# A mixer trunk whose emission planner models TensorE's clock: new branch order and two attention workers

## The chip, the core and the metric

One core of a Trainium2 chip runs the whole program. The time is device microseconds of one execution, the median of three runs. TensorE multiplies 128x128 tiles, VectorE (DVE) and ScalarE (ACT) work elementwise, GpSimd (POOL) does some elementwise work and accumulating DMAs, SyncE (SP) starts the plain DMAs. Each engine takes its instructions strictly in the order in which the program lists them.

## What is computed

Two layers. In each, five branches read the normalised input: a (differential attention), b (dilated attention), c (a diagonal state recurrence, S5), d (compressed, selected and window attention), e (attention into a memory). The outputs are gated, projected, weighted and summed, and a last projection is added to the residual.

```python
for l in range(DEPTH):
    h = rmsnorm(x, norm_g[l])
    proj = h @ w_in[l]            # q, k, v and gate columns of a, b, c, d, e
    ...
    o_a = diff_attention(qa, ka, va, lam, lam_init, diff_subln_g[l])
    o_b = dilated_attention(qb, kb, vb)
    o_c = s5_branch(c_u, ...)
    o_d = nsa_attention(d_q, d_kc, d_vc, d_ks, d_vs, d_kw, d_vw, d_g, ...)
    o_e = memory_attention(e_q, mem, mem_norm_g[l], w_mem_kv[l])
    branches = jnp.stack([o_a * jax.nn.silu(a_z), ..., o_e * jax.nn.silu(e_z)], axis=2)
    y = jnp.einsum('bsnc,ncd->bsnd', branches, w_branch[l])
    gate = jax.nn.sigmoid(h @ w_merge[l] + b_merge[l])
    x = x + (jnp.einsum('bsnd,bsnd->bsd', gate, y)) @ w_out[l]
return rmsnorm(x, final_g)
```

There are 512 tokens of width 1024, 256 memory tokens, four heads of 64 in each attention branch.

## The kernel before

Tokens lie along the free axis, channels along the 128 partitions, so nearly every tile is 128x512. Each float32 operand is split into a high part (a rounded copy) and a low part (the rest), and a product is three matmuls: `mm3` issues high x high, low x high, high x low into one accumulator. A projection of 128 channels is eight such triples, 24 matmuls of 512 columns into an `acc` tile (a PSUM bank). Weights come as pieces of 128x512: a SyncE DMA into `raw`, a ScalarE cast into `whi`, and `wlo` either as a VectorE subtraction or as a ScalarE negated copy to which a GpSimd DMA adds the weights again.

An attention head makes scores in an `sc` tile piece by piece (`causal_exp`: VectorE masks and finds the maximum, ScalarE takes the exponential into `prob`), normalises `prob` on VectorE, and then (`pv`) for three groups of blocks transposes `prob` on TensorE into `pt`, copies it to `ph` on ScalarE, takes the rest `pl` on VectorE, and multiplies both with the values into `o`. `pt` and `ms` (small sums) share the three `sc` buffers. There are three `acc`, three `sc` and two `o` buffers. The compression of d (`compress`, tiles `cxh`, `hd`) takes weight pieces too, but uses a piece up in four narrow matmuls. The recurrence (`s5_operators`, tiles `e`, `p`, `c`) is a chain of small VectorE steps with a few TensorE products (`ms<-e,c`). The memory's keys and values are `mem_kv` (`mh`, `ml`).

The order of all this is not written out. `_trace` runs generators, called streams: the attention workers, the compression, the recurrences, the projections, the trunk (gates, branch projections, output projection) and the memory. It runs first without emitting, to list weight pieces and grants of buffers, then again to emit. Each instruction advances an estimated clock of its engine (`_Engine`, line 223). TensorE's clock `T.now` is the program's: `_Streams.run` (line 321) picks the first stream, by rank, whose wake time has been reached, or else the one that wakes first. So the estimate decides the order in which instructions stand in each engine's queue. Line 243 records every instruction, which is why every row of the profile has L243.

The constants of line 39 on steer it: `ORDER` and `MERGES` list the branches of each layer for the projections and for the trunk, `AFTER` says what the recurrence (`c`) and the memory of layer 1 (`m`) wait for, `RANK` orders the streams, `WORKERS` is the number of heads that may run at once, `PA` holds how many heads of d (or of a's first half) may be left when a projection of a starts, two numbers for each layer.

Of the kernel before, what the change touches and what calls it, by code (L numbers as in the profile page):

```python
# [37 lines left out]
LAT = 100  # L38
ORDER = ('beda', 'edba')
MERGES = ('bedac', 'edbca')  # L40
AFTER = {'s': 'mem', 'c': ('mem', 'dk'), 'm': ('b', 'a')}
RANK = {'att': 1, 'cmp': 1, 'rec': 2, 'ch': 3, 'proj': 4, 'trunk': 5, 'mem': 3}
EARLY = (1, 1)
GO = 4
WORKERS = 3
PA = (4, 4, 2, 4)

MAGIC = 12582912.0
SQ2PI = math.sqrt(2.0 / math.pi)
# [176 lines left out]
class _Engine:  # L226


    def __init__(self, eng, ready, clock, per, fixed):
        self.eng, self.ready, self.clock, self.per, self.fixed = eng, ready, clock or self, per, fixed  # L230
        self.now = 0.0

    def __getattr__(self, name):
        def call(out, *args, **kw):
            ins = [a for a in (*args, *kw.values()) if hasattr(a, "tensor")]
            n = max(math.prod(a.shape[1:]) for a in [out] + ins)
            start = max([self.now, self.clock.now] + [self.ready.get(a.tensor.name, 0.0) for a in ins])
            self.now = start + self.cost(name, n, out, args) + (190 if "accum_out" in kw else 0)
            outs = [out, args[-1]] if name == "tensor_tensor_reduce" else [out, kw.get("accum_out", out)]
            for a in outs:  # L240
                self.ready[a.tensor.name] = self.now + LAT
            if self.eng is not None:
                getattr(self.eng, name)(out, *args, **kw)  # L243

        return call

    def cost(self, name, n, out, args):
        return self.fixed + n * (165 if ALU.pow in args else self.per * (1.5 if name == "tensor_tensor_scan" else 1))


class _Tensor(_Engine):
    def cost(self, name, n, out, args):
        n = math.prod(out.shape[1:])
        if name == "matmul" and args[1].dtype != F32R:
            return 2 * (self.fixed + max(64, 2 * n) * self.per)
        return self.fixed + max(107, n * self.per)


class _Queue(_Engine):
# [150 lines left out]
def _trace(ctx, tc, A, plan):  # L410
# [33 lines left out]
    def take(ring, dt=F32):  # L444
        return rings[AL.get(ring, ring)].take(nm(ring), dt)
# [14 lines left out]
    def slots(n, s, dt=F32R):  # L460
        return [slot(s, dt) for _ in range(n)]
# [16 lines left out]
    def need(*keys):  # L478
        return lambda: all(k in R for k in keys)
# [383 lines left out]

    def mem_kv(l):
        if l == 0:
            yield need("x")
        yield arena.room(18, SPARE)
        raws = slots(4, "mraw", F32)
        for q in range(4):
# [18 lines left out]
        for k in range(KD):  # L888
            yield at(raws[k // 2], cols)
            c = slice(256 * (k % 2), 256 * (k % 2) + 256)  # L890
# [30 lines left out]
        for i in range(2):  # L921
            a = yield from take("acc")
# [10 lines left out]
        for i in range(2):  # L933
            a = yield from take("acc")
# [713 lines left out]
    def s5_operators(l, h):  # L1648
# [43 lines left out]
        def place(b):  # L1692

            x = yield from take("tmp")
            for g in range(4):
                src = bass.AP(kd.tensor, kd.offset + (4 * b + g) * 16 * 240, [[240, 16], [16, 8], [1, 128]])
                SY.dma_start(x[:, 128 * g:128 * g + 128], src)
            yield at(x)
            AC.copy(m2[b].rearrange("p (g c t) -> p g c t", g=4, t=TC), x.rearrange("p (g t c) -> p g c t", g=4, t=TC))
            give("tmp", x, AC.now)  # L1700

        js = [spawn(place(b), RANK["rec"]) for b in range(2)]
        m1 = slots(2, "m1", F32)
# [306 lines left out]
    def memories():  # L2010
        for l in range(L):
            if l:
                yield need(("o", l - 1, "abcde".index(AFTER["m"][l])))
            yield from mem_kv(l)

    def projections():
        for l in range(L):
            yield need(("h", l))
            tabs, which = None, None
            for b in ORDER[l]:  # L2020
# [15 lines left out]
                else:  # L2036
                    for i in range(2):
                        if i == 0 and ORDER[l].index("a") > ORDER[l].index("d"):
                            yield lambda: left.get((l, "d"), 4) <= PA[2 * l]
                        elif i:  # L2040
                            yield lambda: left.get((l, "a", 0), 2) <= PA[2 * l + 1]
                        yield from proj_a(l, i, tabs)
# [9 lines left out]
    def attentions():  # L2052
        while jobs:
            yield from jobs.pop(0)
# [6 lines left out]
    def recurrences():  # L2061
        yield need((AFTER["s"], 0))
        yield from s5_params()
        for l in range(L):
            yield from lambda_params(l)
        for l in range(L):
            yield need((AFTER["c"][l], l) if AFTER["c"][l][0] != "o" else ("o", l, "abcde".index(AFTER["c"][l][1])))
            ys = []
            for h in range(2):
                ops = yield from s5_operators(l, h)  # L2070
                uc = yield from s5_in(l, h)
                ys.append((yield from s5_chunks(l, h, uc, *ops)))
            yield from s5_glu(l, ys)
# [51 lines left out]
    AC.activation(mrep[:, 0:1], mhalf[:, 0:1], AF.Exp)  # L2125
    for _ in range(WORKERS):
        spawn(attentions(), RANK["att"])
    spawn(compression(), RANK["cmp"])
    spawn(recurrences(), RANK["rec"])
    spawn(projections(), RANK["proj"])  # L2130
    spawn(opening(), 1)
    spawn(trunk(), RANK["trunk"])
    spawn(memories(), RANK["mem"])
# [21 lines left out]
```

## Time and profile before

| | us |
|---|---|
| median of three runs (1364.15 to 1365.39) | 1364.4 |
| the profiled execution | 1364.17 |
| its span, first to last instruction | 1362.4 |
| TensorE busy in the span | 1279.9 |
| VectorE busy | 870.1 |
| ScalarE busy | 835.4 |
| GpSimd busy | 407.6 |

The page gives the busy time of each engine. [...] Its waits view sums the idle time of an engine by the tile it was about to write and by the engine and tile it waited for. Its timeline lists single instructions.

### The profile page before, as it was taken

The page shows a single profiled execution, that of the slowest core. Times are in us where ns is not written, and L with a number is a line of the kernel's source. Part 1 is how long each engine was busy: PE and PEld are TensorE (multiplying, and loading weights), DVE is VectorE, ACT ScalarE, POOL GpSimd, SP SyncE. Part 2 cuts the span into 40 slices and gives each one's busy share as a digit, 9 for nine tenths or more (in the row PEclk, how much of TensorE's full clock was granted, in tenths as well). Part 3 has the DMA queues.
Part 4 walks back from the last instruction along what each step waited for, and adds up shares of the span by engine and source line. Part 5 has one row for each costly group of instructions (what it writes and reads, how often), then busy time and mean ns, then how long its engine had stood idle before and what let it go on. Part 6 is the DMA issues. An engine that isn't in the chain of part 4 may idle for free.

```text
span 1362.4 us, 19594 instructions
## 1 busy us (share of the span) xinstructions
PE 1279.9 (94%) x6303; PEld 1051.5 (77%) x6303; DVE 870.1 (64%) x2199; ACT 835.4 (61%) x1699; POOL 407.6 (30%) x523
## 2 busy tenths in 40 slices
PE   5799799999999989999989889999989999999997
PEld 3688677887888778888867567888867888888886
DVE  6978866666787585344457968757877673333442
ACT  6677767757676364644547766757877573434442
POOL 2733323203236235211232354312225222111112
PEclk8999899999999989999989889999989999999998
DMA  7574677736798798676844796656549767656651
GB/s 249 115 164 109 142 188 181 175 95 127 164 187 174 188 202 186 148 189 172 246 112 108 173 218 150 145 128 158 114 113 195 147 139 163 154 133 162 177 171 62
DMA packets 130630, 215.30 MB, mean 158 GB/s; under 512 B 22496, under 2 KB 29792, under 8 KB 130528
## 3 DMA queue, kind: packets, MB, share of 16 engines
q0 software_dynamic: 40896, 74.47, 34.0%
q1 hardware_dynamic: 89632, 139.59, 32.9%
q8 instruction: 49, 0.80, 0.2%
q14 instruction: 53, 0.43, 0.1%
HBM read 190.38 MB, written 23.56 MB: 157 GB/s over the span
## 4 chain that ended last, share of the span: by engine, by line
PE 77%; DVE 12%; ACT 5%; DMA 3%; issue 2%; POOL 0%; SPq 0%; DVEq 0%; ACTq 0%; POOLq 0%
PE acc L243 63%; PE ms L243 4%; PE o L243 3%; PE sc L243 3%; PE pt L243 3%; DVE c L243 2%; DMA raw<-wu 1%; ACT whi L243 1%; DVE x L243 1%; DVE prob L243 1%; DVE tmp L243 1%; ACT prob L243 1%; DVE p L243 1%; DVE wlo L243 1%; DVE rope L243 1%
## 5 line engine op out<-in xcount | busy, mean ns | idle before, releaser
L243 PE MATMUL acc<-hh,whi 128*128 128x512 f32 x1136 | 460.2, 405 | 14.6 <-ACT whi L243 6.5
L243 PE MATMUL acc<-hl,whi 128*128 128x512 f32 x1136 | 449.8, 396 | 4.2 <-DVE hl L243 4.1
L243 PE MATMUL acc<-hh,wlo 128*128 128x512 f32 x1136 | 449.4, 396 | 4.3 <-DVE wlo L243 2.5
L243 ACT CAST whi<-raw 128x512 fp32r<-128x512 f32 x408 | 250.9, 617 | 296.8 <-PE acc L243 249.9
L283 POOL DMA_DIRECT2D wlo<-wu x236 | 210.6, 901 | 643.0 <-ACT wlo L243 512.3
L243 PEld LDWEIGHTS acc<-hh,whi 128*128 128x128 f32 x1136 | 217.5, 191 | 64.4 <-ACT hh L243 9.7
L243 PEld LDWEIGHTS acc<-hh,wlo 128*128 128x128 f32 x1136 | 216.7, 191 | 52.8 <-DVE wlo L243 3.4
L243 PEld LDWEIGHTS acc<-hl,whi 128*128 128x128 f32 x1136 | 217.3, 191 | 48.0 <-DVE hl L243 7.6
L243 DVE TENSOR_TENSOR wlo<-raw,whi 128x512 fp32r<-128x512 f32 x172 | 120.3, 703 | 134.8 <-ACT whi L243 134.3
L243 ACT ACTIVATE wlo<-raw 128x512 fp32r<-128x512 f32 x236 | 148.0, 627 | 4.9 <-DMA raw<-wu 4.3
L243 ACT CAST ph<-pt 128x512 fp32r<-128x512 f32 (+1 forms) x112 | 58.5, 524 | 69.8 <-PE pt L243 68.6
L243 DVE SCALAR_TENSOR_TENSOR gate<-gate,acc 128x512 f32<-128x512 f32 x80 | 54.8, 685 | 72.1 <-ACT gate L243 37.1
L243 ACT ACTIVATE prob<-prob,nb 128x512 f32<-128x512 f32 (+3 forms) x160 | 89.4, 559 | 15.2 <-DVE nb L243 14.5
L243 DVE CUSTOM_DVE_ANT_0 prob<-sc,cst 128x128 f32<-128x128 f32 (+3 forms) x128 | 61.1, 488 | 49.5 <-PE sc L243 48.8
L283 POOL DMA_DIRECT2D mixed<-gate x48 | 44.4, 925 | 154.7 <-DVE gate L243 135.0
L243 DVE TENSOR_TENSOR pl<-pt,ph 128x512 fp32r<-128x512 f32 (+1 forms) x112 | 68.3, 611 | 34.9 <-ACT ph L243 34.4
L243 PE MATMUL acc<-mx,whi 128*128 128x512 f32 (+1 forms) x288 | 81.0, 367 | 0.0
L243 PE MATMUL acc<-bl,whi 128*128 128x512 f32 x160 | 62.9, 393 | 0.7 <-DVE bl L243 0.7
L243 PE MATMUL acc<-bh,whi 128*128 128x512 f32 x160 | 63.6, 397 | 0.0
L243 PE MATMUL acc<-bh,wlo 128*128 128x512 f32 x160 | 62.9, 393 | 0.0
L243 PE MATMUL pt<-cst,prob 128*128 128x128 f32 x384 | 62.3, 279 | 0.0
L243 PEld LDWEIGHTS acc<-mx,whi 128*128 128x128 f32 x288 | 52.0, 189 | 9.2 <-issue 0.3
(318 smaller groups left out, 2092.9 us busy)
## 6 DMA issues: line engine op xcount, KB each, us to landing
raw<-wu SPq DMA_DIRECT2D x408, 256.0 KB, 3.7
wlo<-wu POOLq DMA_DIRECT2D x236, 256.0 KB, 5.3
mixed<-gate POOLq DMA_DIRECT2D x48, 256.0 KB, 4.7
mixed<-gate SPq DMA_DIRECT2D x16, 256.0 KB, 4.0
gate<-mixed SPq DMA_DIRECT2D x16, 256.0 KB, 3.3
x<-xT SPq DMA_DIRECT2D x8, 256.0 KB, 6.0
mraw<-memT SPq DMA_DIRECT2D x8, 256.0 KB, 5.7
tab<-rope SPq DMA_DIRECT2D x8, 256.0 KB, 5.7
```

Of the source, the lines that this page charges most:

```text
L243: getattr(self.eng, name)(out, *args, **kw)
L283: self.eng.dma_start(out, src, accum_op=ALU.add)
```

## The change

The estimate of TensorE gets a second rate. When an instruction starts more than 1200 ns (of the estimate) after the end of the one before it, matmuls cost double until 3400 ns after that start. With this estimate the constants are set anew: two workers instead of three, another `PA`, the recurrence of rank 4 instead of 2, and its start tied to the output of e in layer 0 and to the projections of d in layer 1. `MEM0` has the value that stood in its place. No instruction is written differently; what reaches the engines is another order.

```diff
-AFTER = {'s': 'mem', 'c': ('mem', 'dk'), 'm': ('b', 'a')}
-RANK = {'att': 1, 'cmp': 1, 'rec': 2, 'ch': 3, 'proj': 4, 'trunk': 5, 'mem': 3}
+AFTER = {'s': 'mem', 'c': ('oe', 'pd'), 'm': ('b', 'a')}
+RANK = {'att': 1, 'cmp': 1, 'rec': 4, 'ch': 3, 'proj': 4, 'trunk': 5, 'mem': 3}
...
-WORKERS = 3
-PA = (4, 4, 2, 4)
+WORKERS = 2
+PA = (4, 3, 3, 1)
+MEM0 = 'x'
...
 class _Engine:
...
             start = max([self.now, self.clock.now] + [self.ready.get(a.tensor.name, 0.0) for a in ins])
+            self.wait(start)
             self.now = start + self.cost(name, n, out, args) + (190 if "accum_out" in kw else 0)
+            self.end = self.now
...
 class _Tensor(_Engine):
+    rate, slow = 1, 0.0
+
+    def wait(self, start):
+        if start - self.end > 1200:
+            self.slow = start + 3400
+        self.rate = 2 if start < self.slow else 1
+
     def cost(self, name, n, out, args):
         n = math.prod(out.shape[1:])
         if name == "matmul" and args[1].dtype != F32R:
-            return 2 * (self.fixed + max(64, 2 * n) * self.per)
-        return self.fixed + max(107, n * self.per)
+            return 2 * (self.fixed + max(64, 2 * n) * self.per) * self.rate
+        return (self.fixed + max(107, n * self.per)) * self.rate
```

TensorE's queue has 5654 rows in both programs, the first 146 and the last 933 alike. Six of the 408 weight pieces change from a VectorE subtraction to the way over ScalarE and GpSimd. The rest is order. Three places of TensorE's queue follow; numbers behind a name tell buffers apart, and a `pt` leads to the `ph` and `pl` with the next higher numbers.

The first is in layer 1, at the last head of e, shortly before the compression. `vm` are the memory's values, the first row holds the head's transposes. Before, rows 3091 to 3098:

```order
L243 MATMUL pt_7912<-cst,prob_7752 128x128 x4
L243 MATMUL acc_7841<-hh_6998,whi_7611 128x512
L243 MATMUL acc_7841<-hl_7006,whi_7611 128x512
L243 MATMUL acc_7841<-hh_6998,wlo_7513 128x512
L243 MATMUL o_7776<-ph_7878,vm_5484 128x512
L243 MATMUL o_7776<-pl_7879,vm_5484 128x512
L243 MATMUL o_7860<-ph_7917,vm_5483 128x512
L243 MATMUL o_7860<-pl_7918,vm_5483 128x512
```

Now, rows 3111 to 3122 of the same queue, with this head's transposes (`pt_7928`) at row 3097:

```order
L246 MATMUL acc_7923<-hl_7010,whi_7706 128x512
L246 MATMUL acc_7923<-hh_7002,wlo_7652 128x512
L246 MATMUL acc_7923<-hh_7003,whi_7706 128x512
L246 MATMUL acc_7923<-hl_7011,whi_7706 128x512
L246 MATMUL acc_7923<-hh_7003,wlo_7652 128x512
L246 MATMUL o_7772<-ph_7899,vm_5479 128x512
L246 MATMUL o_7772<-pl_7900,vm_5479 128x512
L246 MATMUL acc_7923<-hh_7004,whi_7706 128x512
L246 MATMUL acc_7923<-hl_7012,whi_7706 128x512
L246 MATMUL acc_7923<-hh_7004,wlo_7652 128x512
L246 MATMUL o_7876<-ph_7934,vm_5478 128x512
L246 MATMUL o_7876<-pl_7935,vm_5478 128x512
```

From the transposes to the head's first product there are 5 rows before and 23 now, 21 of them projection matmuls.

The second is on TensorE in layer 0, inside the memory projection for layer 1 (`mh`, `ml`), where the second half of the recurrence makes its first product (`ms<-e,c`). Before, rows 2002 to 2009:

```order
L243 MATMUL acc_5416<-ml_5212,whi_5238 128x256
L243 MATMUL acc_5416<-mh_5208,wlo_5191 128x256
L243 MATMUL ms_5469<-e_5228,c_5225 32x128
L243 MATMUL ms_5469<-e_5229,c_5225 32x128
L243 MATMUL ms_5469<-e_5228,c_5225 32x128
L243 MATMUL ms_5469<-e_5229,c_5225 32x128
L243 MATMUL ms_5469<-e_5228,c_5225 32x128
L243 MATMUL ms_5469<-e_5229,c_5225 32x128
```

Now, rows 2054 to 2062:

```order
L246 MATMUL acc_5519<-ml_5226,whi_5392 128x256
L246 MATMUL acc_5519<-mh_5222,wlo_5373 128x256
L246 MATMUL acc_5519<-mh_5222,whi_5392 128x256
L246 MATMUL acc_5519<-ml_5226,whi_5392 128x256
L246 MATMUL acc_5519<-mh_5222,wlo_5373 128x256
L246 MATMUL ms_5563<-e_5186,c_5183 32x128
L246 MATMUL ms_5563<-e_5187,c_5183 32x128
L246 MATMUL ms_5563<-e_5186,c_5183 32x128
L246 MATMUL ms_5563<-e_5187,c_5183 32x128
```

The memory projection begins at row 1956 in both; the recurrence's product stands at row 2004 before and at row 2059 now.

The third is on TensorE in layer 1, at the end of d's heads (`dvs` are their values, `dkk` and `dkl` their keys, `b_k` and `bkl` the keys of b). Before, rows 3713 to 3724:

```order
L243 MATMUL pt_9677<-cst,prob_9546 128x128 x4
L243 MATMUL sc_9686<-b_k_9046,b_q_8550 128x384
L243 MATMUL sc_9686<-bkl_9048,b_q_8550 128x384
L243 MATMUL acc_9658<-hh_6995,whi_9409 128x512
L243 MATMUL acc_9658<-hl_7003,whi_9409 128x512
L243 MATMUL acc_9658<-hh_6995,wlo_9388 128x512
L243 MATMUL acc_9658<-hh_6996,whi_9409 128x512
L243 MATMUL acc_9658<-hl_7004,whi_9409 128x512
L243 MATMUL acc_9658<-hh_6996,wlo_9388 128x512
L243 MATMUL o_9570<-ph_9654,dvs_8032 128x384
L243 MATMUL o_9570<-pl_9655,dvs_8032 128x384
L243 MATMUL o_9570<-ph_9654,dvs_8032 128x128
```

Now, rows 3835 to 3846:

```order
L246 MATMUL pt_9906<-cst,prob_9656 128x128 x4
L246 MATMUL pt_9928<-cst,prob_9840 128x128 x4
L246 MATMUL o_9806<-ph_9911,dvs_7917 128x384
L246 MATMUL o_9806<-pl_9912,dvs_7917 128x384
L246 MATMUL o_9806<-ph_9911,dvs_7917 128x128
L246 MATMUL o_9806<-pl_9912,dvs_7917 128x128
L246 MATMUL pt_9941<-cst,prob_9656 128x128 x2
L246 MATMUL o_9652<-ph_9933,dvs_7918 128x512
L246 MATMUL o_9652<-pl_9934,dvs_7918 128x512
L246 MATMUL pt_9949<-cst,prob_9840 128x128 x4
L246 MATMUL o_9806<-ph_9944,dvs_7917 128x256
L246 MATMUL o_9806<-pl_9945,dvs_7917 128x256
```

Before, a projection runs between the heads' transposes and products; now the rows 3833 to 3861 are two heads of d alone, and the rows 3890 to 3917 the last head of d with the first heads of b.

## Rows read from the trace of the kernel before

**Rows 1.** The page, first part: busy us, share of the span and instructions.
```profile
PE 1279.9 (94%) x6303; PEld 1051.5 (77%) x6303; DVE 870.1 (64%) x2199; ACT 835.4 (61%) x1699; POOL 407.6 (30%) x523
```

**Rows 2.** Windows view: length, busy us by engine (records), PEclk, DMA share, GB/s.
```profile
core 0: us, PE busy (x) PEld busy (x) DVE busy (x) ACT busy (x) POOL busy (x), PEclk, DMA share, GB/s
...
138.00:158.00 20.00, 12.90 (x65) 10.20 (x64) 18.32 (x37) 14.19 (x32) 9.53 (x9) 0.83 0.67 147
...
320.00:335.00 15.00, 12.68 (x57) 10.48 (x56) 9.86 (x32) 11.27 (x26) 2.60 (x3) 0.89 0.40 68
...
485.00:508.00 23.00, 18.34 (x114) 15.68 (x114) 18.61 (x57) 14.23 (x32) 5.47 (x7) 0.85 0.93 212
...
752.00:806.00 54.00, 41.89 (x203) 30.80 (x202) 43.48 (x121) 36.05 (x72) 18.58 (x25) 0.85 0.81 195
...
985.00:1016.00 31.00, 25.26 (x129) 19.92 (x128) 23.68 (x49) 23.95 (x52) 9.98 (x9) 0.98 0.50 113
1016.00:1075.00 59.00, 56.30 (x275) 46.25 (x275) 42.80 (x150) 40.98 (x87) 27.47 (x56) 0.93 0.86 185
...
1110.00:1350.00 240.00, 239.95 (x1120) 199.49 (x1119) 96.47 (x162) 104.34 (x178) 42.80 (x48) 1.00 0.58 142
```

**Rows 3.** Waits of PE, 752 to 806: tile, releaser: us, times, longest.
```profile
PE o L243 <- DVE pl L243: 2.7, 1, 2.7
PE pt L243 <- DVE hd L243: 2.2, 1, 2.2
PE ms L243 <- DVE cxh L243: 1.9, 1, 1.9
PE acc L243 <- DMA wlo<-wu: 1.8, 1, 1.8
PE ms L243 <- DMA wlo<-wu: 1.5, 2, 1.0
PE acc L243 <- ACT gf L243: 1.0, 1, 1.0
```

**Rows 4.** Timeline of DVE before that pl: start us, us, engine, line, operation.
```profile
752.70 2.37 DVE L243 TENSOR_TENSOR dqn<-rope,dqn 64x512 fp32r<-64x512 f32 x2
755.11 0.69 DVE L243 TENSOR_TENSOR pl<-pt,ph 128x512 fp32r<-128x512 f32 x1
```

**Rows 5.** Waits of PE, 485 to 508.
```profile
PE ms L243 <- issue: 2.3, 1, 2.3
PE ms L243 <- DVE e L243: 1.8, 1, 1.8
```

**Rows 6.** Timeline of PE near 324; in brackets the idle time before and its releaser.
```profile
323.97 0.47 PE L243 MATMUL acc<-hh,whi 128*128 128x512 f32 x1 [2.32 <-DVE vs L243]
```

**Rows 7.** Waits of PE, 138 to 158.
```profile
PE o L243 <- DVE pl L243: 3.6, 2, 2.5
PE acc L243 <- DVE wlo L243: 2.5, 1, 2.5
PE ms L243 <- DVE cxh L243: 0.9, 1, 0.9
```

**Rows 8.** Timelines of DVE and PE before 1016.
```profile
1010.48 0.27 DVE L243 TENSOR_TENSOR c<-p,s5ar 128x64 f32<-128x64 f32 x1 [6.61 <-ACT e L243]
...
1015.54 0.58 PE L243 MATMUL o<-pl,vs 128*128 128x256 f32 x1 [4.24 <-DVE pl L243]
```

**Rows 9.** Timeline of an unhindered turnaround, transposes to pl, near 729.
```profile
728.79 0.60 PE L243 MATMUL pt<-cst,prob 128*128 128x128 f32 x4
...
729.42 0.59 ACT L243 CAST ph<-pt 128x512 fp32r<-128x512 f32 x1 [1.50 <-PE pt L243]
...
730.04 0.69 DVE L243 TENSOR_TENSOR pl<-pt,ph 128x512 fp32r<-128x512 f32 x1 [0.49 <-ACT ph L243]
```

**Rows 10.** Timeline of a b head: last score product, normalising of its four pieces.
```profile
955.15 0.40 PE L243 MATMUL sc<-bkl,b_q 128*128 128x512 f32 x1
...
959.01 1.33 DVE L243 TENSOR_SCALAR prob<-prob,rec 128x128 f32<-128x128 f32 x4
```

**Rows 11.** The page, costliest groups: busy us, mean ns, idle before and its releaser.
```profile
L243 ACT ACTIVATE wlo<-raw 128x512 fp32r<-128x512 f32 x236 | 148.0, 627 | 4.9 <-DMA raw<-wu 4.3
```

More of the change, by code (lines that the diff above doesn't have):

```diff
@@ L230, in __init__ @@
         self.eng, self.ready, self.clock, self.per, self.fixed = eng, ready, clock or self, per, fixed
-        self.now = 0.0
+        self.now = self.end = 0.0
     def __getattr__(self, name):
@@ L245, in __getattr__ @@
         return call
+    def wait(self, start):
+        pass
     def cost(self, name, n, out, args):
@@ L251, with wait @@
 class _Tensor(_Engine):
+    rate, slow = 1, 0.0
+    def wait(self, start):
+        if start - self.end > 1200:
+            self.slow = start + 3400
+        self.rate = 2 if start < self.slow else 1
     def cost(self, name, n, out, args):
@@ L865, in mem_kv @@
         if l == 0:
-            yield need("x")
+            yield need(MEM0)
         yield arena.room(18, SPARE)
```

## Prediction

> **What bounds the kernel now.** TensorE does. On the profile's page it is busy 1279.9 of 1362.4 us, the next engine, VectorE, 870.1 [rows 1]. Every instruction of TensorE stays, so only two things can move the end: time in which TensorE waits, and time in which its matmuls run at half rate. I therefore read the windows view next, cut at the places where the granted clock is below 1.00 [rows 2]. Read each row as length minus PE busy (idle), then as one minus the clock (time lost to half rate, to be weighted with the busy share). In the long row 1110 to 1350, where the order stays, TensorE has no idle and a clock of 1.00, at 240/1120 = 0.21 us per matmul record, most of them 512 columns wide: that is the pace without loss.
>
> The price of each lossy stretch [rows 2], idle plus half rate: 752 to 806 has 54 - 41.9 = 12.1 idle and 0.15 x 54 x 0.78 = 6.3, together 18.4 us; 138 to 158 has 7.1 + 2.2 = 9.3; 320 to 335 has 2.3 + 1.4 = 3.7; 485 to 508 has 4.7 + 2.8 = 7.5; 985 to 1075 (two rows) has 8.4 + 4.4 = 12.8. That is 51.7 us in the part of the program that the change reorders. The opening (the first 146 rows of TensorE), the boundary between the layers, and all from TensorE's row 4721 on stand as before and keep their cost.
>
> **The change part by part.** The new estimate emits nothing. What reaches the chip is another order and other workers. The base is the profiled execution, 1364.2 us (span 1362.4 and 1.8 around it), 0.2 below the median of 1364.4.
>
> 1. Layer 1, compression (752 to 806). The waits view names the cause of each wait [rows 3]. The worst, 2.7 us, is the last head of e: its transposes are followed by three projection matmuls and two products, then by the product that needs pl. VectorE's queue held two dqn subtractions of 2.37 us together in front of that pl [rows 4]. In the new order 21 projection matmuls (some 4.5 us at the pace above) and two products stand between, and VectorE has that pl ahead of its dqn pair. The same holds for hd (2.2 us; the transposes of the recurrence, which stood right behind the row that made VectorE copy hd, now come a hundred rows later), cxh (1.9 us; eighteen rows now stand where eight did) and gf (1.0 us). These 7.8 us go. The waits for wlo (1.8 and 1.5) stay: a compression product uses a weight piece up in four narrow matmuls as before, and nothing loads earlier. Half rate falls in proportion, 6.3 x 7.8/12.1 = 4.1. **-11.9 us**, bounds -18.4 (all of it) and -4 (the pl and cxh waits alone, if VectorE is late for the others).
>
> 2. Recurrence of layer 0, second half (485 to 508). TensorE reaches the first product of e and c before VectorE has made e: 2.3 us put down to issue and 1.8 to e [rows 5]. In the new order that product stands 55 rows later, behind 49 further rows of the memory projection, of 256 columns, and 6 projection matmuls (49 x 0.107 + 6 x 0.214 = 6.5 us at the pace above), while VectorE's queue ahead of e is as long as before. Both waits are covered; nothing that waits is queued behind. **-7.5 us**, bounds -7.5 and 0.
>
> 3. Layer 0, accumulators (320 to 335). A gate projection waits 2.3 us for VectorE to empty a transposed a_v tile, the third accumulator [rows 6]. Before, 27 rows stand between those transposes and the projection, now 53. **-3.7 us**, bound 0.
>
> 4. Layer 0, heads of e and compression (138 to 158). Causes: pl 3.6, wlo 2.5, cxh 0.9 [rows 7]. With two workers instead of three fewer softmaxes crowd VectorE, which was busy 18.3 of 20 us [rows 2], and from the first instruction of the compression's input to the last cxh it has 23 instructions instead of 36. But the second half of the compression, spread among projections before, is now one run of 37 rows with only the last e head in it. One stretch gets better, another one worse: **0**, bounds -5 and +7.
>
> 5. Late layer 1 (985 to 1075). The 4.24 us wait for pl is a queue again: VectorE stood 6.61 us on a recurrence step whose input e ScalarE had not copied, with pl behind it [rows 8]. The same kind of step is still there, now in other company, and a_1's projections move behind two heads of a. I take half of 12.8: **-6**, bounds -12 and 0.
>
> 6. The new cost. In layer 1 e's gate projections are used up at TensorE's row 3832, b's projections before that, and a's first starts at row 3862, while two workers sit in d's last two heads. Rows 3833 to 3861 and 3890 to 3917 hold no projection at all. A turnaround from transposes through ScalarE's ph and VectorE's pl takes 730.73 - 728.79 = 1.94 us when nothing is in the way [rows 9]. Eight of them stand there with only 0.9 to 1.2 us of other rows between: 1.0, 0.85, 0.75, 0.85, 0.9, 1.0, 0.75, 1.0 us of wait, 7.1 in all. Once, the first transposes of a b head come 1.3 us behind its last score product; from a score product to the last normalised piece it took 960.34 - 955.15 = 5.2 us [rows 10]; 3.9 are missing, of which the neighbours hide some 1.4: 2.5. Together 9.6 us, and half rate in the proportion of 752 to 806 (6.3/12.1): 5.0. **+14.6**, bounds +4 (the waits overlap) and +21 (see the second rival).
>
> 7. Six more weight halves go through ScalarE (0.63 us each [rows 11]) and a GpSimd add instead of a VectorE subtraction: 3.8 us of an engine with 39% idle, hidden by it; without that cover it would be those 3.8. **0**. For places that I have not priced, waits that every new order brings (the first e head of layer 1 now has its transposes nine projection matmuls behind its last score): **+3**, bounds 0 and +8.
>
> Sum: -11.9 - 7.5 - 3.7 + 0 - 6 + 14.6 + 0 + 3 = -11.5, so 1364.2 - 11.5 = **1352.7 us**.
>
> **Clock.** The traces show half rate after some waits and none after others of the same size: 985 to 1016 idles 5.7 us at a clock of 0.98, 138 to 158 idles 7.1 at 0.83 [rows 2]. [...]
>
> **The rivals.**
> First, the waits only move (no change). VectorE works in order and has the same 870 us to do, so a pl that is no longer late in one place is late at the next. For it: steps 1, 4 and 5 are all queues of VectorE. Against it: in 752 to 806 VectorE itself stood still for 10 of 54 us [rows 2], so the order can repair it. If steps 1 and 5 give half, and step 2 stays, the sum is -11.5 + 6 + 3 = -2.5: 1361.7, at the edge of no change.
>
> Second, slower: runs without projections cost more than I give them. Where TensorE's order holds only products that hang on VectorE's and ScalarE's last result, every delay of these two shows. The old run of that kind (41 rows inside 138 to 158) cost 9.3 us, 0.23 for each row. The new order has three runs that the old one spread: the second compression of layer 0 (37 rows) and the two of step 6 (29 and 28), 94 rows, 21.3 us instead of 14.6. The first compression of layer 1 is such a run still, so step 1 gives its lower bound of 4, and step 5 nothing: -4 - 7.5 - 3.7 + 21.3 + 3 = +9.1, 1373.3. With the other steps as in my sum it decides against the change from 26 us on (14.6 + 11.5). Against it: in step 6 two heads interleave, where a single one stood before.
>
> Third, all goes: step 5 whole, step 6 at its lower bound: -11.5 - 6 - 10.6 = -28.1, 1336.1 at the best.
>
> That the estimate's clock is off (it halves after any wait over 1.2 us) is no rival of its own: the order is chosen once, and only the order runs.
>
> **How the numbers follow.** Forecast (1344 to 1361) 0.56; third rival 0.12; no change 0.12; slower 0.20. A measurement of this kernel tells about 0.2%, or 2.7 us, from no change. So faster 0.68, same 0.12, slower 0.20. The range runs from 1337 (steps 1, 5 and 6 near their good bounds) to 1370 (just short of the second rival).
>
> **What would show it.** Step 1: no wait of TensorE for pl, hd or cxh over 1 us between the boundary of the layers and the first d scores, and that stretch some 10 us shorter for its work. Step 2: no wait at the product of e and c in layer 0. Step 6: a run of waits for pl, each about 1 us, at the end of d's heads in layer 1, with the clock below 1.00 behind it. I am wrong if that run costs over 20 us, if the second compression of layer 0 waits for weights by more than 5 us, or if waits for pl turn up among a's heads, where I expect none.

## The result: slower, with the gains and the new cost where they were forecast

The changed kernel takes 1378.3 us (median of four executions, 1375.0 to 1380.9) against 1364.9 of the kernel before (1364.2 to 1366.2): 1.0096 of it, interval 1.0071 to 1.0121. The forecast was 1352.7, the range 1337 to 1370. The sign is that of the second rival, the mechanism, as will be seen, is not. (The lists of branches, `ORDER` and `MERGES`, are the same in both kernels: the order that is new is that of rows.)

The profiled execution took 1380.9 us, its span is 1379.1, 16.7 more than before. From the page of the changed kernel, the part that answers to [rows 1]:

```profile
PE 1288.3 (93%) x6303; PEld 1052.7 (76%) x6303; DVE 869.5 (63%) x2193; ACT 837.6 (61%) x1705; POOL 417.7 (30%) x529
```

TensorE is busy 8.4 us longer with the same 6303 records and idle 8.3 us longer. Its granted clock over the span is 0.966 against 0.968, some 5 to 7 us more at half rate, so at most 3 of the 8.4 us are that; the rest is open. (Half rate is a granted clock of 0.50. From 968 to 971 us of the changed kernel the trace shows 0.50, and projection matmuls of 512 columns that follow each other start 0.42 to 0.43 us apart; from 972 to 975 it shows 1.00, and they start 0.22 to 0.24 us apart. Of the trace's 1379 slices of 1 us 1273 show 1.00 and 81 show 0.50.) GpSimd has 10 us more to do, for the six weight pieces; no other engine has more to speak of. The windows view gives the places (columns as in [rows 2]):

```profile
core 0: us, PE busy (x) PEld busy (x) DVE busy (x) ACT busy (x) POOL busy (x), PEclk, DMA share, GB/s
...
214.00:235.00 21.00, 15.69 (x73) 12.81 (x71) 12.39 (x29) 11.60 (x22) 1.71 (x2) 0.84 0.49 123
...
495.00:512.00 17.00, 16.54 (x117) 14.43 (x117) 12.12 (x31) 12.28 (x28) 2.62 (x3) 1.00 0.98 236
...
792.00:822.00 30.00, 24.04 (x130) 18.06 (x129) 27.81 (x58) 20.35 (x39) 14.88 (x15) 1.00 0.86 207
...
925.00:950.00 25.00, 22.57 (x114) 18.38 (x114) 15.80 (x54) 15.36 (x39) 3.53 (x4) 0.93 0.55 132
950.00:975.00 25.00, 19.56 (x75) 14.89 (x75) 17.03 (x42) 16.60 (x37) 3.51 (x3) 0.73 0.12 37
```

Look at the second row first: there the recurrence makes its first product of e and c in layer 0, and the 4.7 us of idle time that 485 to 508 had before [rows 2] are gone. The last two rows are the stretch of step 6, with 7.9 us idle. The first row is a place that the forecast does not mention.

To set the two traces side by side I priced every row of TensorE: for each kind of row (tiles and shape) the median time to the next row in the trace of before. What a place takes beyond the sum of its rows' prices is its loss. Since both programs have the same rows, losses can be compared from place to place. The table is worked out so, for the two profiled executions. They are the slowest of the changed kernel's four and nearly the fastest of the kernel before, so some 3 of the 16.7 us between them are scatter: the medians differ by 13.4.

| TensorE's rows, about | step | loss before | loss after | difference | forecast |
|---|---|---|---|---|---|
| 1 to 480, opening | | 34.9 | 35.8 | +0.9 | 0 |
| 480 to 763, compression of layer 0 | 4 | 10.5 | 10.1 | -0.4 | 0 |
| 763 to 850, a's first projections | none | 1.5 | 7.5 | **+6.0** | none |
| 850 to 1213 | none | -1.9 | 0.1 | +2.0 | none |
| 1213 to 1388 | 3 | 2.9 | -0.2 | -3.1 | -3.7 |
| 1388 to 1903, a's heads, layer 0 | none | 0.0 | 5.9 | **+5.9** | none |
| 1903 to 2208, recurrence and memory | 2 | 6.7 | 0.8 | -5.9 | -7.5 |
| 2208 to 3034, boundary, e's scores | none | 3.9 | 5.5 | +1.6 | none |
| 3034 to 3414, compression of layer 1 | 1 | 22.3 | 12.1 | -10.2 | -11.9 |
| 3414 to 3763 | none | -2.6 | 0.8 | +3.4 | none |
| 3763 to 4027, last heads of d | 6 | -2.1 | 15.8 | **+17.9** | +14.6 |
| 4027 to 4380 | 5 | 11.3 | 3.5 | -7.8 | -6 |
| 4380 to 4550, a's second half | none | 1.1 | 8.2 | **+7.1** | none |
| rest | | | | -0.4 | 0 |

Steps 1 to 6 sum to -9.5 us, against -14.5 in the forecast. All else, the opening and the rest included, sums to +26.5, against +3.

### The profile page after: what moved, and what is told of

It reads as the page before. It is cut to its first block, busy times and chain, and to the rows that moved or that the text cites. A ratio compares the mean times of both kernels' runs of the same rounds, so it can differ in the third digit from the quotient of the medians.

```text
span 1379.1 us, 19590 instructions
## 1 busy us (share of the span) xinstructions
PE 1288.3 (93%) x6303; PEld 1052.7 (76%) x6303; DVE 869.5 (63%) x2193; ACT 837.6 (61%) x1705; POOL 417.7 (30%) x529
## 4 chain that ended last, share of the span: by engine, by line
PE 64%; DVE 9%; issue 4%; ACT 4%; DMA 2%; POOL 1%; DVEq 0%; POOLq 0%; ACTq 0%; SPq 0%
PE acc L246 53%; PE o L246 3%; PE ms L246 3%; PE pt L246 2%; PE sc L246 2%; DVE c L246 2%; DVE tmp L246 1%; DVE prob L246 1%; ACT whi L246 1%; DVE rope L246 1%; DMA uc<-ud 1%; DVE pl L246 1%; DVE x L246 1%; ACT dst L246 1%; DVE r L246 1%
## 5 line engine op out<-in xcount | busy, mean ns | idle before, releaser
L298 POOL DMA_DIRECT2D wlo<-wu x242 | 216.6, 903 | 652.6 <-ACT wlo L246 524.2
L246 DVE TENSOR_TENSOR wlo<-raw,whi 128x512 fp32r<-128x512 f32 x166 | 114.9, 695 | 117.6 <-ACT whi L246 116.5
L246 ACT ACTIVATE wlo<-raw 128x512 fp32r<-128x512 f32 x242 | 151.7, 627 | 9.8 <-DMA raw<-wu 9.0
L246 ACT ACTIVATE prob<-prob,nb 128x128 f32<-128x128 f32 (+3 forms) x160 | 89.5, 560 | 22.1 <-DVE nb L246 21.3
L246 PE MATMUL pt<-cst,prob 128*128 128x128 f32 x384 | 66.2, 286 | 6.1 <-DVE prob L246 6.1
L246 PEld LDWEIGHTS pt<-cst,prob 128*128 128x128 f32 x384 | 48.2, 145 | 18.9 <-DVE prob L246 4.7
```

What stands on the lines that cost most here:

```text
L298: self.eng.dma_start(out, src, accum_op=ALU.add)
```

## Experiments

Ratios are to the kernel before, measured next to it. Only the lines that matter are shown of each edit.

**Does the loss sit in places that add up?** One layer from each kernel. The workers and the halved rate were made to depend on the layer:

```diff
-WORKERS = 2
+WORKERS = (3, 2)
+CLK = (0, 1)
...
-        if start - self.end > 1200:
+        if self.on and start - self.end > 1200:
```

> Layer 0 stands in the order of the kernel before (three workers, no halved rate; only the recurrence's rank differs), layer 1 from TensorE's row 2829 on exactly as in the changed kernel. Theory A, the losses are where the two profiles show them and add up: layer 0 gives back 5.6 us, so some 11 us slower than before, 1376. Rival, the extra time of the changed kernel is loss of clock that follows from one layer into the next or from one execution to another: then this is not between the two kernels, but near one of them (1365 or 1378).

Measured 1.0065 (1.0047 to 1.0083), 1372.9 us. The other half has WORKERS (2, 3), CLK (1, 0) and the old values of the other constants:

> The other half: layer 0 in the changed order, layer 1 from row 2842 on in the order of before. Theory A: +5.6 us, 1370.5, with a wait of 5 us of TensorE for the sigmoid of a gate at its row 832 and one of about 3 us for uc at row 1784. Rival (the two waits are accidents of the one profiled execution, the transfer's above all): 1365 to 1367.

Measured 1.0084 (1.0067 to 1.0100), 1375.7 us. Both intervals lie above 1, so neither layer alone is innocent, and the rival of the second falls. By time alone the rival of the first doesn't: its interval meets that of the changed kernel (1.0071 to 1.0121), and the second ratio lies inside it. The traces speak against it. Priced in the same way, the rows of layer 1 lose 51 us in the first of the two and 55 in the changed kernel, and place by place the traces repeat themselves: the stretch of step 6 loses 13.8 us there and 15.8 in the changed kernel, before -2.1. At row 832 TensorE waits 5.31 us in the second, as in the changed kernel; for uc it waits 1.5 us there, not 3. The second result is larger than 5.6 us because that kernel kept rank 2 and the old start for the recurrence: its loss between rows 1903 and 2208 is 6.4 us, in the changed kernel 0.8. So step 2's gain comes from the recurrence's new constants (the rank is tested alone below), and the rest of the new layer 0 costs some 11 us.

**Workers or the halved rate?** The changed kernel with `self.slow = start` in place of `start + 3400`:

> All constants of the change, the estimate without the halved rate. Theory B, the cost comes from two workers and not from the halved rate, which only repairs some of it: in layer 1 a stretch of 16.1 us of work without a projection (rows 3811 to 3886) instead of 6.1 and 6.5 us, so 17.4 us x 16.1/12.6 = 22 us there, about 1383, slower than the changed kernel. Rival, the halved rate made the new waits (it thinks TensorE later than it is and so hands it too little in front): this one is faster than the changed kernel, 1366 to 1372.

Measured 1.0183 (1.0163 to 1.0203), 1388.0 us: theory B by the time. By its trace layer 1 loses 66 us (55 in the changed kernel) and layer 0 46 (51 in the changed kernel). The theory's total came out, its arithmetic did not: the run without projections at the place of step 6 loses 16.9 us, hardly more than the 15.8 of the changed kernel, and two single waits stand elsewhere, of 8.5 us at a gate projection (for VectorE's tmp) and of 7.4 us at a head's scores (for VectorE's rotated tile). So in layer 1 the new estimate repairs a part of what two workers do, and in layer 0 it does harm. That was tested by itself, the kernel before with two workers in layer 0 alone:

> The kernel before with two workers in layer 0, three in layer 1, the estimate without the halved rate. Layer 1 is that of before to the row. Theory J: in layer 0 the halved rate, not the two workers, makes the new waits; in the profile of the kernel without it (no_clock) layer 0 had lost 4.1 us less than before at 420 us of work, the changed kernel 11.3 us more. So 0.997 of before. Rival, two workers cost the 11 us: 1.008.

Measured 0.9953 (0.9940 to 0.9965): theory J, with a little more gain than it said. Two workers are good for layer 0, and the halved rate is what spoils it. The kernel with the new layer 0 and the old layer 1 (1.0084) differs from this one in a single constant, CLK = (1, 0) for (0, 0), and their layers 1 have the same rows of TensorE. The halved rate in layer 0 thus costs 1.3%, some 18 us, more than the whole change loses. The first 1902 rows of TensorE are the same set in both, only ordered otherwise (2160 records). Up to their ends, with the halved rate and without (columns as in [rows 2]):

```profile
0.00:478.30 478.30, 435.40 (x2160) 353.99 (x2160) 345.94 (x924) 325.70 (x699) 164.91 (x192) 0.96 0.70 159
0.00:464.00 464.00, 434.03 (x2160) 353.70 (x2161) 344.53 (x924) 326.71 (x698) 165.97 (x193) 0.96 0.72 164
```

At the same row the changed kernel is at 479.2 us, the changed kernel without the halved rate at 463.9, the kernel before at 467.9. That is 11.3 us behind the kernel before with the halved rate, and 4 ahead of it without. (With the recurrence's new constants the 15.3 us between the first two of these are not all kept: at row 2417 they are 4.9 us, the 5 us of layer 0 above.) The windows of the kernel with two workers in layer 0 for the places of [rows 2] show where it gains:

```profile
core 0: us, PE busy (x) PEld busy (x) DVE busy (x) ACT busy (x) POOL busy (x), PEclk, DMA share, GB/s
130.00:160.00 30.00, 27.13 (x141) 22.28 (x140) 26.74 (x57) 21.70 (x50) 11.54 (x10) 0.94 0.57 143
206.00:227.00 21.00, 17.30 (x70) 13.80 (x70) 14.80 (x34) 17.63 (x31) 5.04 (x6) 0.84 0.58 126
312.00:330.00 18.00, 18.00 (x90) 15.16 (x89) 13.26 (x45) 13.12 (x32) 5.86 (x7) 1.00 0.75 150
```

The compression (first row) has 2.9 us idle in 30, where 138 to 158 alone had 7.1 [rows 2], and step 3's wait (last row) is gone. The middle row is the place of the gate, which loses 6 us in this kernel too (7.5 in the changed kernel, 1.5 before): most of that one belongs to the two workers.

**The first wait that I missed, row 832.** TensorE's and ScalarE's rows of the changed kernel around it, then VectorE's:

```profile
225.62 0.79 PE L246 MATMUL acc<-hh,whi 128*128 128x512 f32 x1 [5.31 <-ACT gate L246]
...
217.50 3.13 ACT L246 CAST dst<-rope 32x512 fp32r<-32x512 f32 x5
223.44 0.37 ACT L246 CAST vs<-acc 128x256 fp32r<-128x256 f32 x1 [2.82 <-DVE vs L246]
223.84 0.63 ACT L246 ACTIVATE wlo<-raw 128x512 fp32r<-128x512 f32 x1
224.38 0.60 ACT L246 CAST whi<-raw 128x512 fp32r<-128x512 f32 x1
224.88 0.68 ACT L246 ACTIVATE gate<-acc,hb 128x512 f32<-128x512 f32 x1
...
218.66 0.69 DVE L246 TENSOR_TENSOR tmp<-tmp,cmx 128x512 f32<-128x512 f32 x1
219.38 2.06 DVE L246 TENSOR_TENSOR dst<-rope,dst 32x512 fp32r<-32x512 f32 x3
...
221.67 0.68 DVE L246 TENSOR_TENSOR dst<-rope,dst 32x512 fp32r<-32x512 f32 x1
222.38 0.69 DVE L246 TENSOR_TENSOR wlo<-raw,whi 128x512 fp32r<-128x512 f32 x1
222.99 0.41 DVE L246 TENSOR_TENSOR vs<-acc,vs 128x256 fp32r<-128x256 f32 x1
```

Read it from the end. TensorE begins a gate projection and needs one of the three accumulators. One is freed by the sigmoid (`gate<-acc`, 224.88), which had been ready to run when the projection before it ended. It stands behind the second cast of a pair of value tiles (`vs`), and that cast waited 2.82 us for VectorE's subtraction in the first. VectorE had the scores of d's compressed head and the rotated tiles of a (`dst<-rope`) before it. The wait at row 4443 is of the same kind: four of a's casts, 2.5 us, stand right in front of the sigmoid:

```profile
1096.47 0.50 PE L246 MATMUL acc<-hh,whi 128*128 128x512 f32 x1 [2.59 <-ACT gate L246]
...
1092.81 2.50 ACT L246 CAST dst<-rope 32x512 fp32r<-32x512 f32 x4
1095.33 0.37 ACT L246 CAST vs<-acc 128x256 fp32r<-128x256 f32 x1
1095.73 0.69 ACT L246 ACTIVATE gate<-acc,hb 128x512 f32<-128x512 f32 x1
```

The experiment changes ScalarE's queue and nothing else, by issuing an instruction at another place while the planner counts it where it was:

```diff
+                if j == 0 and AC.eng is not None:
+                    AC.eng.copy(vs[1][:, :, :, 0:64], v[:, 2:4])
...
             AC.activation(g, a, AF.Tanh, bias=hb[l][:, 8 * n + m:8 * n + m + 1], scale=0.5)
+            while LATER:
+                AC.eng.copy(*LATER.pop(0))
```

> The changed kernel; TensorE's and VectorE's rows stay word for word, only ScalarE's queue is changed at two kinds of places. The second of the two casts of a value tile (vs) stands right behind the first, so that it no longer waits for VectorE; and at the end of layer 1 five casts of a's rotated keys stand behind a gate's sigmoid instead of in front of it. Theory D, TensorE waits at its rows 832 and 4443 because the sigmoid that frees its accumulator is stuck behind these casts: the wait at 832 falls from 5.3 to about 2.7 us, that at 4443 from 2.6 to under 0.5, together 5 us, and as much again if the half rate behind them goes too: 1368 to 1373. Rival, the accumulator is held by VectorE's work just as long: both waits stay, 1378.

Measured 1.0073 (1.0055 to 1.0090), 1373.4 us, just above the upper end of theory D. The interval meets that of the changed kernel, so the gain is read from the trace. Its TensorE:

```profile
223.11 0.50 PE L247 MATMUL acc<-hh,whi 128*128 128x512 f32 x1 [2.40 <-ACT gate L247]
...
1088.82 1.05 PE L247 MATMUL ms<-cst,tmp 128*128 128x2 f32 x8 [2.51 <-ACT tmp L247]
```

In layer 0 the wait shrank to 2.4 us, as forecast, and the place loses 3.2 us less. In layer 1 the wait for the gate went, and three rows later a wait of 2.5 us for another ScalarE row took its place: the casts had only been passed on. At row 832 the cause is shown for 2.9 of the 5.3 us; the 2.4 that are left were not taken apart. At row 4443 the casts are shown, but the gain at that end is not there.

**PA.** The gate at row 4443 comes with a's second half. Projecting it earlier, as before:

> The changed kernel with PA = (4, 3, 3, 4), so that a's second half of layer 1 is projected as early as before; TensorE's rows differ from the changed kernel's only from 4426 to 4720. Theory C: the 2.6 us wait for a gate's sigmoid at row 4443 comes from the casts of a's rotated keys that ScalarE has in front of it, and these casts now stand elsewhere: the 6.0 us lost there go, 1372. Rival: the same casts meet another gate's sigmoid or the heads of a wait for them: no change, 1378.

Measured 1.0132 (1.0110 to 1.0153), 1382.0 us: no gain, the rival. TensorE's rows differ from 4074 on, not from 4426, so step 5's stretch is another one too. Theory C's mechanism holds at its place, where the loss falls by 7.7 us (4380 to 4550), but the rows 4027 to 4380 lose 9.6 us more. The casts moved there, and the longest wait is for another gate's sigmoid, which three of them (1.9 us) and other rows of ScalarE precede:

```profile
1046.92 0.80 PE L246 MATMUL acc<-hh,whi 128*128 128x512 f32 x1 [5.15 <-ACT gate L246]
```

**The stretch of step 6.** First, is it the clock? Idle products were put into its two longest waits:

```diff
         pt = yield from take("pt")
+        if warm and T.eng is not None:
+            hh, hl, _ = R["h", 1]
+            for k in range(warm):
+                T.eng.matmul(pt, hl[k % 4][:, :128], hh[k % 4], start=True, stop=True)
```

> The changed kernel with 19 products of 512 columns more on TensorE, whose result nobody reads: 7 in front of the transposes at row 3836 (TensorE waits 1.7 us there) and 12 in front of those at row 3898 (3.0 us). All other rows stay. At full rate one takes 0.23 us, so they fill the two waits (1.6 and 2.8 us). Theory E, half rate follows from these two waits and costs by itself: TensorE runs at 0.50 from 957.9 to 971.4 us and from 936.8 to 940.5, which costs some 5.8 + 1.7 us; with the waits filled that goes, 1371. Rival, the short waits that are left (1.3, 0.7, 0.4 us) bring the clock down as well, or the added products cost their own 4.3 us: 1378 to 1383.

Measured 1.0114 (1.0096 to 1.0132), 1379.6 us: no gain. The windows of 930 to 945 and 950 to 975, of the changed kernel and then of this one:

```profile
930.00:945.00 15.00, 12.56 (x62) 9.83 (x61) 10.29 (x32) 9.26 (x25) 0.88 (x1) 0.89 0.51 141
950.00:975.00 25.00, 19.56 (x75) 14.89 (x75) 17.03 (x42) 16.60 (x37) 3.51 (x3) 0.73 0.12 37
```

```profile
930.00:945.00 15.00, 14.02 (x70) 10.48 (x70) 10.71 (x32) 10.16 (x27) 0.88 (x1) 1.00 0.53 142
950.00:975.00 25.00, 21.19 (x92) 16.21 (x91) 18.92 (x49) 17.67 (x41) 4.34 (x4) 0.86 0.13 38
```

The products did keep the clock up, wholly in the first window and in part of the second. They did not make the transposes late: TensorE still waits 0.3 us for prob behind the twelve. Yet from the transposes at row 3835 to row 3928 the changed kernel takes 37.0 us and this one 35.4. In these two windows half rate, as one minus the clock times the busy time, went from 0.11 x 12.6 + 0.27 x 19.6 = 6.7 us to 0.14 x 21.2 = 3.0; of these 3.7 us the stretch gave back 1.6. In this stretch, where TensorE waits for VectorE's and ScalarE's turnarounds, more than half of the loss at half rate ran inside the waits, by an estimate from these 3.7 and 1.6 us.

Second, is it the missing work between the heads? A third worker joins in layer 1 once d's compressed head is taken, with the old layer 0 and PA (the edit against the kernel with the old layer 0 and the new layer 1):

```diff
-        while jobs and w < WORKERS[jobs[0][0]]:
+        while jobs:
+            if w == 2 and len(jobs) <= 17:
+                yield lambda: len(jobs) <= 12
...
```

> Layer 0 in the order of before (with the recurrence's new rank). Layer 1 with the halved rate and the recurrence's new start as in the changed kernel, but a third worker joins once the first head of d is taken, and PA has the values of before. Up to TensorE's row 3500 it is the kernel with the old layer 0 and the new layer 1 (1372.9). Theory F, the loss at the end of d's heads comes from two heads with nothing between them: summed over the heads' turnarounds of layer 1, what is missing to 1.94 us is 5.9 us here, 13.0 in the changed kernel, 3.6 in the one before, so 17.4 us there become about 4: 1359 to 1361, faster than before. Rival, the third worker crowds VectorE as before and the waits only go elsewhere: 1368 or more.

Measured 1.0041 (1.0026 to 1.0055), 1370.3 us, slower than theory F and than the kernel before. The profiled execution is the fastest of nine (1364.8 us), so its trace shows the places and not the whole of the loss. At its place the theory holds in part: the stretch loses 7.7 us instead of 13.8 with the same layer 0. But a new wait, the longest of all, stands behind it:

```profile
1018.51 1.12 PE L247 MATMUL pt<-cst,p 128*128 128x128 f32 x4 [10.60 <-DVE p L247]
...
1009.78 0.27 DVE L247 TENSOR_TENSOR c<-p,s5ar 128x64 f32<-128x64 f32 x1 [4.64 <-ACT e L247]
...
1007.87 1.24 ACT L247 CAST dst<-rope 32x512 fp32r<-32x512 f32 x2
1009.14 0.62 ACT L247 COPY e<-c 64x512 f32<-64x512 f32 x1
1009.66 2.53 ACT L247 CAST dst<-rope 32x512 fp32r<-32x512 f32 x4
```

TensorE waits for p; VectorE had stood 4.64 us for ScalarE's copy of e, in front of which ScalarE had two of a's casts (1.24 us) and other rows. So at most 4.6 of the 10.6 us hang on the copy: from 1009.8 to 1018.4 us VectorE is busy with its own rows, the recurrence's steps among those of three heads. The place loses 15.6 us. With the recurrence started as before:

> As the kernel with the third worker from d on, with the recurrence of layer 1 started as before (with d's keys, not with its projections). What is missing in the turnarounds is 6.0 us. Theory F: 1359 to 1362, the same. Rival, the recurrence's start matters by itself (its VectorE steps then fall on the compression): slower by over 3 us.

Measured 1.0076 (1.0057 to 1.0096): the rival. The stretch of step 6 costs almost nothing then (0.4 us between 3855 and 3945), but four other places lose 5 to 10 us each. And with the casts behind the recurrence's copies (rank 3, one by one):

> The kernel with the third worker from d on (1370.3), with one edit: in layer 1 the casts of a's rotated keys and queries come with rank 3 instead of 1 and one by one, so that ScalarE takes the recurrence's copies first. Theory G, ScalarE's burst of these casts is what TensorE waits for next to a's projections, whatever stands behind it: there the recurrence's copy of e, with a wait of 10.6 us and 15.6 us lost. With the copy in front of the casts that wait is under 2 us, and 8 casts in front of one gate's sigmoid cost at most 5: 1358 to 1363. Rival, VectorE, busy with three heads, makes the recurrence late by itself: 1368 to 1371.

Measured 1.0062 (1.0042 to 1.0082), not faster: the 10.6 us became 3.9, not under 2, and the place's loss 6.3. That is the way theory G went, but the time is the rival's: two other places lost 4 to 5 us more. The same edit on the kernel before:

> The kernel before with the recurrence's rank 4 and, in layer 1, the casts of a's rotated keys and queries at rank 3 and one by one. TensorE's rows of layer 1 change from 4202 on besides those of the rank. Theory G: the 4.2 us wait for pl near 1015 us, where VectorE stood behind a copy of e that ScalarE had not made, stays or goes with the casts, and of the 9.9 us lost between 1005 and 1050 us half goes: 1356 to 1360. Rival, the copy was late for other reasons than the casts: as with the rank alone.

Measured 1.0003 (0.9989 to 1.0018): not theory G, and by the median 3.3 us behind the rank alone, though the intervals meet. The wait for a pl there fell to 2.0 us, and one of 4.3 us at the recurrence's transposes took its place. What hangs on these casts in one order hangs on something else in the next.

**Step 2 and step 3 alone.** One constant of the change on the kernel before (`'rec': 4`):

> The kernel before with one constant changed: the recurrence's rank 4 instead of 2. TensorE's rows differ in two stretches only, 2132 to 2634 in layer 0 and 3377 to 3629 in layer 1. Theory H, step 2 of the prediction is right by itself: the wait for e at the first product of e and c in layer 0 (rows 2004 and 2005, 4.1 us and the half rate behind it, 7 us in all) is covered, and the later products of the recurrence take back 1.5 us (its p at row 2135) and 2 us of half rate: 1361. Rival, the recurrence, now behind everything else, is late at the gates of c and in layer 1: 1364 or more.

Measured 0.9981 (0.9967 to 0.9995): theory H, and a kernel faster than both, by little. (The two stretches, counted in rows as elsewhere here, are 1938 to 2417 and 3304 to 3734.) The wait for e is gone; the rows 1903 to 2208 lose 3.2 us less than before, and 5.9 less in the changed kernel. Then the pairs of value tiles, whose second half stands behind a's rotated tiles in both queues:

```diff
+                if j == 0 and V.eng is not None:
+                    V.eng.tensor_tensor(vs[1][:, :, :, 64:128], v[:, 2:4], vs[1][:, :, :, 0:64].bitcast(F32), ALU.subtract)
```

> The kernel before with the recurrence's rank 4 (rank_alone, 0.998 of before), and in each pair of value tiles (vs) the second cast on ScalarE and the second subtraction on VectorE stand right behind the first, before the casts and subtractions of a's rotated keys and queries. TensorE's rows are those of rank_alone. Theory G: step 3's wait, 2.3 us at row 1285 for the third accumulator, is these rotated tiles too; ScalarE spends 2.5 us on them between the two casts, VectorE 2.8 us between the two subtractions. The wait goes with its half rate, 3.7 us: 0.995 of before. Rival, the next accumulator (a gate's, freed at about the same time) keeps TensorE there: as rank_alone, 0.998.

Measured 0.9946 (0.9934 to 0.9958), 1355.5 us against 1363.5, the ratio of theory G. TensorE no longer waits for `vs` [rows 6]; two windows of its trace, step 3's and step 2's:

```profile
312.00:330.00 18.00, 16.38 (x88) 13.80 (x88) 12.28 (x32) 15.06 (x33) 6.64 (x7) 1.00 0.70 135
478.00:515.00 37.00, 34.79 (x201) 28.68 (x200) 29.02 (x79) 24.97 (x50) 11.68 (x18) 1.00 0.87 203
```

A wait of 1.6 us for a pl, four rows on, took a part of it back, so the place gave 2.2 of the 3.7 us. The rest of the gain over the rank alone lies scattered in places of about 1 us, of either sign, and its cause is open. Both edits for the order of two workers in layer 0:

> As two_workers_l0, with the second cast and subtraction of each pair of value tiles right behind the first. Theories G and J: 0.994 to 0.997 of before, the accumulator held by the pair being free earlier. Rival: no difference from two_workers_l0.

Measured 0.9946 (0.9930 to 0.9963), 1356.1 us. Its interval holds the ratio of the kernel with two workers in layer 0 alone (0.9953), so here the pairs show nothing that can be told: two workers had already taken step 3's wait away.

## Why the prediction was wrong

**Step 7 failed.** "For places that I have not priced ... +3, bounds 0 and +8" stood for every wait that a new order brings. The traces show 26.5 us. The 23.5 us between are most of the 28 between the forecast and the profiled execution; the other 5 are in the steps that were priced. Three places make most of it: the gate at row 832 (+6.0), a's heads of layer 0 (+5.9) and the gate at row 4443 (+7.1 with its surroundings). The two gates have a source in common that I had in hand: step 3's wait for `vs` [rows 6], where a's rotated tiles stand in front on ScalarE (2.5 us of casts) and on VectorE (2.8 us). I read it as a single wait that goes away, not as a burst that hits whatever TensorE needs next to a's projections, and I searched the new order for the heads' turnarounds alone. A new order must be read at every hand-over: for each accumulator that TensorE takes, who frees it, and what stands before that row on its engine. I had no such list, so the 3 us were a guess, and the bounds around them too.

The third place, 1388 to 1903, goes with the halved rate. These rows, all but five of 515 alike, take 123.9 to 126.2 us in the five kernels whose layer 0 was ordered with it, and 120.0 in the three ordered with two workers and without it. In the changed kernel the waits there are for a pl, for tmp and for the recurrence's input uc, which comes back by a DMA:

```profile
397.11 0.45 PE L246 MATMUL o<-pl,vs 128*128 128x384 f32 x1 [1.29 <-DVE pl L246]
...
420.29 0.69 PE L246 MATMUL ms<-tmp,cst 8*128 8x512 f32 x1 [1.06 <-DVE tmp L246]
...
450.10 0.28 PE L246 MATMUL ms<-uc,m 128*64 128x64 f32 x2 [2.83 <-DMA uc<-ud]
```

The wait for uc was 2.1, 1.6, 1.5 and 0.6 us in four other kernels with these rows, so it explains some of the scatter. Why the order with the halved rate brings the other two is open. The prediction let the estimate's clock pass as no rival, since "only the order runs". But the order is what the estimate makes, and with the halved rate it made a worse one in layer 0 and, with these constants, a better one in layer 1.

**Step 1**: right in size. The waits for cxh and gf are gone (those for hd stayed, 2.1 us in two), that for the last e head's pl fell from 2.7 to 1.3 us, but 1.3 for ph came beside it, and two waits for a weight's rest by VectorE (2.2 and 1.4 us) took the place of those by DMA. In 792 to 822 TensorE idles 6.0 us at a clock of 1.00. At 842.6 a wait of 2.5 us for the recurrence's p followed, which step 1 had put a hundred rows further on without asking what would be late there. So two of the forecast's own signs failed: waits for pl and hd of 1.28 us each, where it said none over 1, and the wait for a pl among a's heads (1.29 us, above), where it expected none.

**Step 2**: right; the rank alone takes the wait away and gives 3.2 of the 5.9 us. **Step 3**: right in size. **Step 4**: right, 0 of two opposite terms (-2.2 and +1.7). **Step 5**: -7.8, a little better than half.

**Step 6**: the place was right and the size nearly (+17.9 for +14.6, inside the bounds), the inner working was not. I expected eight waits for pl near 1 us. There are two long ones for prob, in front of the first transposes of a head:

```profile
936.75 1.37 PE L246 MATMUL pt<-cst,prob 128*128 128x128 f32 x4 [1.73 <-DVE prob L246]
...
957.87 1.46 PE L246 MATMUL pt<-cst,prob 128*128 128x128 f32 x4 [3.00 <-DVE prob L246]
...
963.04 0.79 PE L246 MATMUL o<-pl,vs 128*128 128x512 f32 x1 [1.28 <-DVE pl L246]
```

Idle time was 7.9 us for my 9.6; half rate, at one minus the clock times the busy share, 0.07 x 25 x 0.90 + 0.27 x 25 x 0.78 = 6.8 for my 5.0. That the sum of these two comes to 14.7 is partly luck: the idle products gave back less than half of the half rate that they removed, so the 6.8 is not all a cost of its own.

**The rivals.** The second came nearest in time (1373.3), by "runs without projections cost more". Step 6 did cost more than its term (the rival's own price for these 57 rows, 0.23 each, was 13, less than the term), the second compression of layer 0 +1.7 where it priced 8.5, and steps 1 and 5 gave their gains, against it. The kernel is slower by places that no rival names. In the stretch of step 6 the clock fell to 0.73 at 5.4 us idle in 25 (950 to 975), but 792 to 822 idles 6.0 us in 30, in waits of up to 2.2 us, at 1.00. So the amount of idle time alone does not tell which stretch runs at half rate, as [rows 2] showed before.

## What to carry to other kernels

When an order is chosen anew, the waits that it removes can be priced one by one from the old trace, and steps 1 to 5 came out within 2 us each here; of the waits that it brings only those at the heads' turnarounds were priced (step 6), and the others were nine times what was set aside. Look for bursts on the engines beside the bottleneck (here the casts of a pair of rotated tiles, 18 of 0.62 us, 11 us of ScalarE) and ask in the new order what TensorE needs next to each of them. Change a planner's estimate and its constants one at a time: faster kernels came from single parts of the change, the rank (0.9981) and two workers in layer 0 without the halved rate (0.9953), and from an edit that is not in it, the second half of a pair issued right behind the first (0.9946 with the rank).

## What the runs showed of the hardware

The waits for engines that were compared repeated to some hundredths of a microsecond between executions and kernels with the same rows: 5.31 us at row 832 in four kernels, 3.00 or 3.01 at row 3898 in four, 1.28 at row 3905 in the same four. The wait for the DMA of uc did not (2.83, 2.1, 1.6, 1.5, 0.6 us at row 1784).

Half rate in the stretch of step 6, which waits for other engines, cost 1.6 us where one minus the clock, times the busy time, said 3.7 (the idle products).

At the place of row 832 ScalarE's cast from the second half of an accumulator waited 2.82 us for VectorE's subtraction from the first half, though they touch different columns and tiles. With the cast issued in front of that subtraction TensorE's wait there fell from 5.31 to 2.40 us, by 2.9. The 2.82 us are thus what the order of the two cost here, where the engine that went first was late; why the cast has to wait for the subtraction was not shown.
